# Stick-breaking attention with its stages moved apart, its sums from split operands, and seven of the weight halves made on GpSimd

## The chip, the core and the metric

The kernel runs on one core of a Trainium2 chip. The metric is the device time of one execution in microseconds. The work is spread over the engines that the profile calls PE (TensorE, matrix products), ACT (ScalarE), DVE (VectorE), POOL (GpSimd) and SP (SyncE, here the queue that issues the DMAs). Each engine works through its own queue in order and waits on semaphores where it needs what another engine makes.

## What is computed

Two transformer blocks run one after the other on 256 tokens of width 1024, in float32. The part that matters here is the first block's stick-breaking attention, with 8 heads of width 64, and the RWKV branch beside it. The reference, cut to that:

```python
def stick_breaking_attention(q, k, v):
    for i in range(S // Q_BLOCK):                 # Q_BLOCK = 128, S = 256
        ...
        z = jnp.einsum('bqhd,bkhd->bhqk', qb, kb).astype(jnp.float32) * scale
        strict = s_idx < t_idx
        log_fail = jnp.where(strict, jax.nn.log_sigmoid(-z), 0.0)
        after = lax.cumsum(log_fail, axis=3, reverse=True) - log_fail
        w = jnp.where(strict, jnp.exp(jax.nn.log_sigmoid(z) + after), 0.0)
        outs.append(jnp.einsum('bhqk,bkhd->bqhd', w.astype(vb.dtype), vb))

def first_block(x, ...):
    h = rms_norm(x, norm_mix_pre[l])
    proj = h @ w_in[l]                            # 1024 x 5376
    ...
    o_sb = stick_breaking_attention(q, k, v)
    o_rw = rwkv7_time_mix(p_rw, ...)              # a recurrence over the tokens
    merged = gates[..., :D] * (o_sb @ w_sb_out[l]) + gates[..., D:] * (o_rw @ w_rw_out[l])
    ...
```

## The kernel before

**Weights.** Every weight matrix is streamed in slabs of 128 x 1024 floats (four times 128 rows by 256 columns). The method `slab` loads one (a DMA into `wraw`, 512 KB), rounds it on ACT to `whi` (line 182), and takes the rest on DVE as `wlo = wraw - whi` (line 183). Buffers: three of `wraw`, four each of `whi` and `wlo`; `fetch` keeps three slabs ahead of PE. A block is what PE does with one slab: 24 matmuls of 256 columns, three products (hi by hi, hi by lo, lo by hi) for each of eight pairs. The input matrix comes as `w_rw` (14 slabs), `w_sb` (12 slabs: two pairs each for q, k and v in that order) and `w_gate` (16 slabs), two slabs to a group of 256 output columns, the lower half being rows 512 to 1023 (odd slab numbers). Here they are called sb0 to sb11 and g0 to g15.

**Weaving.** `weave` takes a generator, and each call of `next_slab`, so each block, advances it by one step. While PE works on the v slabs sb8 to sb11 and the gate slabs g0 to g7 (twelve blocks, numbered 0 to 11 here), the steps are the attention's: `sb_scores(j)`, `sb_weights(j)`, `sb_values(j)` for four pairs of heads j. With `staggered(..., apart=2)` scores stand ahead of blocks 0, 2, 4, 6, weights ahead of 2, 4, 6, 8, and values ahead of 4, 6, 8, 10; at a block with all three, values come first and scores last.

**The stages.** `sb_scores` makes the masked logits of a pair in PSUM (`pz`, two buffers of the pool `zz`), then |z|, exp and log on ACT (Abs, Exp, Ln), then on DVE `zm = max(z, 0) + log(...)` (line 784). `sb_weights` adds to the same `pz` the suffix sums of `zm` by two matmuls of 384 and two of 128 columns against the constants `suffix` and `negones`, all plain float32, and takes the exponential on ACT into `ab`. `sb_values` multiplies with v into `po`, copies it to `of` and splits that into `sh`, `sl`.

**Beside it** DVE inverts 16 x 16 triangles for the RWKV branch: fifteen pairs of `pr` and `TF` (lines 718 and 719) in a chain that starts when the matrix `Q` has landed, then two steps of `rows` (`prw`, lines 736 and 739), the first two products against `Q`, the other two against `low`, which goes out and back by DMA after ACT's copy `aux` (line 722) of the finished `TF`. A scheduler sets the order of each engine's queue from the program; what results is a fixed row of instructions on each engine.

Of the kernel before, what the change touches and what calls it, by code (L numbers as in the profile page):

```python
# [43 lines left out]
for _n, _c in VECS:  # L44
# [47 lines left out]
class Net:  # L92
    def __init__(self, ctx, tc, io):
        self.tc, self.nc, self.io = tc, tc.nc, io
        self.last_table = None
        self.queue, self.ready = [], []
        self.t2 = 3
        self.side = None
        nc = self.nc
        pool = lambda name, bufs=1, **k: ctx.enter_context(tc.tile_pool(name=name, bufs=bufs, **k))  # L100
        self.keep = pool("keep")
        self.pr = pool("wraw", 3)
        self.ph = pool("whi", 4)
# [70 lines left out]
    def slab(self, name, i):  # L174
        nc = self.nc
        off, k0, m, c0 = slabs(*WEIGHTS[name])[i]
        w = m * width(name)
        raw = self.pr.tile([P, SW], F32, tag="wraw", name="wraw")
        hi = self.ph.tile([P, SW], F32R, tag="whi", name="whi")
        lo = self.pl.tile([P, SW], F32R, tag="wlo", name="wlo")  # L180
        nc.sync.dma_start(raw[:, :w], self.io[name][off:off + P * w].rearrange("(p n) -> p n", p=P))
        nc.scalar.copy(hi[:, :w], raw[:, :w])  # L182
        nc.vector.tensor_sub(lo[:, :w], raw[:, :w], hi[:, :w].bitcast(F32))  # L183
        h3 = hi[:, :w].rearrange("p (k c) -> p k c", k=m)
        l3 = lo[:, :w].rearrange("p (k c) -> p k c", k=m)
        return h3, l3, k0, m
# [231 lines left out]
def first(n):  # L418
    nc, tc = n.nc, n.tc
    with ExitStack() as ctx:  # L420
# [81 lines left out]
        n.normed(tmp, xp, r, "norm_mix_pre", n.xh, n.xl)  # L502
        shifted(2, kf, 2, r)
        start.close()
        b4 = ctx.enter_context(tc.tile_pool(name="b4", bufs=8))


        n.table("sigmoid_and_others")
# [183 lines left out]

        def sb_v(g):
            ps = n.group("w_sb", 4 + g, n.xh, n.xl, tok=True)
            nc.vector.tensor_copy(vs_[:, :, g * 256:(g + 1) * 256], ps)

# [58 lines left out]
            for q in range(2):  # L755
                nc.vector.tensor_mul(MG[h][q][:, :, 0, :], MG[h][q][:, :, 0, :], low)

        sbf = tmp.tile([P, 384], F32, tag="t30", name="sbf", bufs=4)
        o, w = COFF["sbmask"]
        nc.scalar.dma_start(sbf, n.io["cst"][:, o:o + w])  # L760
        sbm = one.tile([P, 384], BF16, name="sbm")
        nc.scalar.copy(sbm, sbf)
        idb = one.tile([P, P], BF16, name="idb")
        nc.scalar.copy(idb, n.c("ident"))
        sh = b4.tile([P, NP, T], F32R, tag="b4", name="sh")
# [6 lines left out]
        def sb_scores(j):  # L772
            p = pz[j] = n.zz("pz")
            for o, kc, qc in ((slice(0, T), slice(0, P), slice(0, T)), (slice(T, T + P), slice(P, T), slice(P, T))):
                for r_, rr in enumerate(half):
                    n.mm(p[:, r_, o], ks[rr, j, kc], qs[rr, j, qc], start=kc.start == 0)
            for r_ in range(2):
                n.mm(p[:, r_, :384], idb, sbm, start=False)
            z = tmp.tile([P, 2, 384], F32, tag="t30", name="zm", bufs=4)
            ab = tmp.tile([P, 2, 384], F32, tag="t30", name="ab", bufs=4)  # L780
            nc.scalar.activation(ab, p[:, :, :384], AF.Abs)
            n.act(ab, ab, AF.Exp, scale=-1.0)
            n.act(ab, ab, AF.Ln, bias=n.one)
            nc.vector.scalar_tensor_tensor(z, p[:, :, :384], 0.0, ab, op0=ALU.max, op1=ALU.add)
            zm[j] = z, ab

        def sb_weights(j):
            p, (z, ab) = pz[j], zm[j]
            for r_ in range(2):
                n.mm(p[:, r_, :384], n.c("suffix"), z[:, r_, :], start=False)  # L790
            for r_ in range(2):
                n.mm(p[:, r_, P:T], n.c("negones"), z[:, r_, T:384], start=False)
            n.act(ab, p[:, :, :384], AF.Exp)

        def sb_values(j):
            wt = zm[j][1]
            po = n.sx("po")
            for t, o, wc in ((0, slice(0, T), slice(0, T)), (1, slice(P, T), slice(T, 384))):
                for r_, rr in enumerate(half):
                    i = 2 * j + r_  # L800
                    n.mm(po[rr, o], vs_[:, t, 64 * i:64 * i + 64], wt[:, r_, wc], start=t == 0)
            of = tmp.tile([P, T], F32, tag="c2", name="of", bufs=3)
            nc.vector.tensor_copy(of, po[:, :T])
            n.split(of, sh[:, j, :], sl[:, j, :])

        early.close()
        n.psum(sb, zz=2, sx=2)
        n.weave(staggered(NP, sb_values, sb_weights, sb_scores, apart=2))
        sb_v(0)
        sb_v(1)  # L810
        gr = [B(f"gate{i}") for i in range(4)]

        def gate(g, final):

            i, h = g // 2, 2 * (g % 2)
            ps = n.group("w_gate", g, n.xh, n.xl)
            if final:
                sig(g, ps)
            else:
                nc.scalar.copy(gr[i][:, h:h + 2, :], ps)  # L820
# [23 lines left out]
        def solve(h):  # L844
# [114 lines left out]
        def normalized():  # L959
# [479 lines left out]
```

## Time and profile before

| | |
|---|---|
| median of 3 runs | 851.95 us (851.76 to 854.29) |
| the profiled execution's own time | 853.44 us |
| its span, first to last instruction | 851.7 us |
| PE busy | 829.5 us (97%), 6508 matmuls |
| DVE busy | 565.3 us (66%), 790 instructions |
| ACT busy | 464.9 us (55%), 714 instructions |
| POOL busy | 5.4 us (1%), 14 instructions |
| chain that ended last, by engine | PE 90%, DVE 5%, DMA 2%, ACT 2%, issue 1% |
| granted clock of TensorE, mean | 0.994 |

A matmul's end is modelled, so a busy PE isn't PE at its peak; what counts is when each group of matmuls starts. The busy shares are means over stages with different limits: over the whole span DVE is busy two thirds of the time, but between 105 and 143 us it is hardly ever idle. The timeline merges like instructions that follow one another; its first two columns are the start and the time from there to the end, and square brackets hold the idle time before and what ended it.

### The profile page before, as it was taken

To read this page: it belongs to the slowest core of one execution; us is meant where nothing else is said; L and a number is where in the kernel's file an instruction comes from. 1 tells how busy PE (TensorE), PEld (TensorE's weight loads), DVE (VectorE), ACT (ScalarE), POOL (GpSimd) and SP (SyncE) were. 2 spreads that over 40 slices of the span, in tenths; PEclk is the share of its full clock that TensorE was granted. 3 is DMA by queue.
4 is the path that set the end of the run, shared out by engine and by line. 5 is a ranking of instruction groups with operands and counts; after the bars stand their busy time and mean duration, and the time that the engine had idled before them with its cause. 6 is when DMAs were issued, how large, how long until landed. Compare 5 with 4: busy or idle time off the path is not lost.

```text
span 851.7 us, 15759 instructions
## 1 busy us (share of the span) xinstructions
PE 829.5 (97%) x6508; PEld 788.4 (93%) x6508; DVE 565.3 (66%) x790; ACT 464.9 (55%) x714; POOL 5.4 (1%) x14
## 2 busy tenths in 40 slices
PE   5999998999999999999999999999999999999996
PEld 5798987999999999999999998999999999988884
DVE  6858689455888776666545876689576666654543
ACT  6497355643577654445445657457455565553432
POOL 0001001000000000000000000000000000000000
PEclk9999999999999999999999999999999999999999
DMA  8434443542464765555555564455524555556551
GB/s 283 149 133 159 136 130 117 160 140 87 145 251 144 225 189 183 195 177 197 173 187 186 158 202 149 148 174 184 188 95 153 176 172 177 193 178 193 179 193 50
DMA packets 44631, 142.88 MB, mean 168 GB/s; under 512 B 8976, under 2 KB 9744, under 8 KB 44304
## 3 DMA queue, kind: packets, MB, share of 16 engines
q1 hardware_dynamic: 43840, 139.25, 50.7%
q10 hardware_dynamic: 720, 2.63, 0.8%
q8 instruction: 51, 0.84, 0.4%
q14 instruction: 20, 0.16, 0.1%
HBM read 139.17 MB, written 2.69 MB: 167 GB/s over the span
## 4 chain that ended last, share of the span: by engine, by line
PE 90%; DVE 5%; DMA 2%; ACT 2%; issue 1%; SPq 0%; ACTq 0%; DVEq 0%
PE mm L247 68%; PE mm L262 11%; DMA wraw<-in_w_rw 2%; PE pz L262 2%; DVE wlo L183 1%; PE po L262 1%; ACT whi L182 1%; PE px L262 1%; PE mgnh L262 1%; PE nv L262 1%; DVE prw L736 1%; PE kv L247 1%; PE ssum L262 1%; DVE pr L718 1%; DVE TF L719 0%
## 5 line engine op out<-in xcount | busy, mean ns | idle before, releaser
L183 DVE TENSOR_TENSOR wlo<-wraw,whi 128x1024 fp32r<-128x1024 f32 x254 | 308.2, 1215 | 198.8 <-ACT whi L182 197.3
L182 ACT CAST whi<-wraw 128x1024 fp32r<-128x1024 f32 x254 | 264.8, 1044 | 291.5 <-PE mm L247 174.9
L247 PE MATMUL mm<-xh,whi 128*128 128x256 f32 x1120 | 319.3, 285 | 0.0
L247 PE MATMUL mm<-xh,wlo 128*128 128x256 f32 x1120 | 316.1, 282 | 1.8 <-DVE wlo L183 1.8
L247 PE MATMUL mm<-xl,whi 128*128 128x256 f32 x1120 | 316.1, 282 | 0.0
L247 PEld LDWEIGHTS mm<-xh,whi 128*128 128x128 f32 x1120 | 212.0, 189 | 3.8 <-issue 2.2
L247 PEld LDWEIGHTS mm<-xh,wlo 128*128 128x128 f32 x1120 | 211.8, 189 | 2.9 <-DVE wlo L183 2.2
L247 PEld LDWEIGHTS mm<-xl,whi 128*128 128x128 f32 x1120 | 211.8, 189 | 0.9 <-issue 0.7
L262 PE MATMUL mm<-whi,ah 128*128 128x512 f32 x128 | 50.6, 395 | 0.0
L262 PE MATMUL mm<-whi,al 128*128 128x512 f32 x128 | 50.6, 395 | 0.0
L262 PE MATMUL mm<-wlo,ah 128*128 128x512 f32 x128 | 50.6, 395 | 0.0
L247 PE MATMUL mm<-fh,whi 128*128 128x256 f32 x176 | 49.1, 279 | 0.0
L247 PE MATMUL mm<-fl,whi 128*128 128x256 f32 x176 | 49.1, 279 | 0.0
L247 PE MATMUL mm<-fh,wlo 128*128 128x256 f32 x176 | 49.1, 279 | 0.0
L247 PEld LDWEIGHTS mm<-fl,whi 128*128 128x128 f32 x176 | 33.1, 188 | 0.0
L247 PEld LDWEIGHTS mm<-fh,wlo 128*128 128x128 f32 x176 | 33.1, 188 | 0.0
L247 PEld LDWEIGHTS mm<-fh,whi 128*128 128x128 f32 x176 | 33.1, 188 | 0.0
L262 PEld LDWEIGHTS mm<-whi,al 128*128 128x128 f32 x128 | 24.1, 188 | 5.8
L262 PEld LDWEIGHTS mm<-wlo,ah 128*128 128x128 f32 x128 | 24.1, 188 | 5.8
L262 PEld LDWEIGHTS mm<-whi,ah 128*128 128x128 f32 x128 | 24.1, 188 | 5.7
L247 PE MATMUL rw<-gh,whi 128*128 128x256 f32 x48 | 14.2, 296 | 9.0 <-ACT whi L182 9.0
L247 PE MATMUL mm<-memh,whi 128*128 128x256 f32 x64 | 18.8, 294 | 0.0
(349 smaller groups left out, 1379.9 us busy)
## 6 DMA issues: line engine op xcount, KB each, us to landing
wraw<-in_w_up SPq DMA_DIRECT2D x32, 512.0 KB, 3.5
wraw<-in_w_down SPq DMA_DIRECT2D x32, 512.0 KB, 4.3
wraw<-in_w_in SPq DMA_DIRECT2D x24, 512.0 KB, 4.2
wraw<-in_w_ffn_gate SPq DMA_DIRECT2D x22, 512.0 KB, 3.8
wraw<-in_w_ffn_up SPq DMA_DIRECT2D x22, 512.0 KB, 3.3
wraw<-in_w_ffn_down SPq DMA_DIRECT2D x20, 512.0 KB, 3.5
wraw<-in_w_gate SPq DMA_DIRECT2D x16, 512.0 KB, 3.3
wraw<-in_w_kv_mem SPq DMA_DIRECT2D x16, 512.0 KB, 3.3
```

The lines of the kernel that those rows point to most:

```text
L182: nc.scalar.copy(hi[:, :w], raw[:, :w])
L183: nc.vector.tensor_sub(lo[:, :w], raw[:, :w], hi[:, :w].bitcast(F32))
L247: self.nc.tensor.matmul(ps[:, c, :], lhsT, rhs, start=first, stop=last, skip_group_check=True)
L262: self.nc.tensor.matmul(out, lhsT, rhs, start=start, stop=stop, skip_group_check=True)
L718: nc.vector.tensor_mul(pr[:, :, :, :t + 1], tri[:, :, :, :t + 1], q)
L736: nc.vector.tensor_mul(pr, left[:, r:r + 4, :].rearrange("p r (o i) -> p r o i", o=1).to_broadcast([P, 4, 16, 16]), right.rearrange("p (o ...
```

## The change

1. **GpSimd makes `wlo` of seven slabs**: sb3, sb5, sb7, sb9, sb11, g1 and g3. DVE makes the others as before.
2. **The stages stand further apart**: scores ahead of blocks 0, 2, 4, 6 as before, weights ahead of 3, 5, 7, 9 (three blocks after their scores instead of two), values ahead of 5, 7, 9, 11.
3. **The sums take split operands**: the result of line 784 goes into `ab` itself and is split into `zhi` (a cast on ACT) and `zlo` (a subtraction on DVE); the suffix sums are eight fp32r matmuls in place of four float32 ones, against `sums`, an fp32r copy of the two constants, whose columns hold only 0 and -1. The exponential goes to a new tile `wt`.
4. **Small moves**: the copies of v from PSUM go from DVE to ACT; `po` is split without the copy `of`; the constants are loaded in another order (the load at the start on ACT's queue is 640 columns wide in place of 384, the one on SP's queue 960 in place of 1216); the pool `t30` has six buffers for four and `b4` seven for eight, and the gate tiles are taken when first needed.

```diff
 class Net:
+        self.others = {"w_sb": (3, 5, 7, 9, 11), "w_gate": (1, 3)}
...
         nc.scalar.copy(hi[:, :w], raw[:, :w])
-        nc.vector.tensor_sub(lo[:, :w], raw[:, :w], hi[:, :w].bitcast(F32))
+        engine = nc.gpsimd if i in self.others.get(name, ()) else nc.vector
+        engine.tensor_sub(lo[:, :w], raw[:, :w], hi[:, :w].bitcast(F32))
...
         def sb_v(g):
-            nc.vector.tensor_copy(vs_[:, :, g * 256:(g + 1) * 256], ps)
+            nc.scalar.copy(vs_[:, :, g * 256:(g + 1) * 256], ps)
...
+        sums = tmp.tile([P, 256], F32R, tag="t1", name="sums", bufs=1)
+        nc.scalar.copy(sums, sbf[:, 384:])
...
         def sb_scores(j):
-            z = tmp.tile([P, 2, 384], F32, tag="t30", name="zm", bufs=4)
-            ab = tmp.tile([P, 2, 384], F32, tag="t30", name="ab", bufs=4)
+            ab = tmp.tile([P, 2, 384], F32, tag="t30", name="ab", bufs=6)
+            hi = tmp.tile([P, 2, 384], F32R, tag="t30", name="zhi", bufs=6)
+            lo = tmp.tile([P, 2, 384], F32R, tag="t30", name="zlo", bufs=6)
             nc.scalar.activation(ab, p[:, :, :384], AF.Abs)
             n.act(ab, ab, AF.Exp, scale=-1.0)
             n.act(ab, ab, AF.Ln, bias=n.one)
-            nc.vector.scalar_tensor_tensor(z, p[:, :, :384], 0.0, ab, op0=ALU.max, op1=ALU.add)
+            nc.vector.scalar_tensor_tensor(ab, p[:, :, :384], 0.0, ab, op0=ALU.max, op1=ALU.add)
+            n.split(ab, hi, lo)
...
         def sb_weights(j):
             for r_ in range(2):
-                n.mm(p[:, r_, :384], n.c("suffix"), z[:, r_, :], start=False)
+                for z in (hi, lo):
+                    n.mm(p[:, r_, :384], sums[:, :P], z[:, r_, :], start=False)
             for r_ in range(2):
-                n.mm(p[:, r_, P:T], n.c("negones"), z[:, r_, T:384], start=False)
-            n.act(ab, p[:, :, :384], AF.Exp)
+                for z in (hi, lo):
+                    n.mm(p[:, r_, P:T], sums[:, P:], z[:, r_, T:384], start=False)
+            wt = zm[j] = tmp.tile([P, 2, 384], F32, tag="t30", name="wt", bufs=6)
+            n.act(wt, p[:, :, :384], AF.Exp)
...
         def sb_values(j):
-            of = tmp.tile([P, T], F32, tag="c2", name="of", bufs=3)
-            nc.vector.tensor_copy(of, po[:, :T])
-            n.split(of, sh[:, j, :], sl[:, j, :])
+            n.split(po[:, :T], sh[:, j, :], sl[:, j, :])
...
-        n.weave(staggered(NP, sb_values, sb_weights, sb_scores, apart=2))
+        def attention():
+            for b in range(2 * NP + 4):
+                for stage, first in ((sb_values, 5), (sb_weights, 3), (sb_scores, 0)):
+                    j = (b - first) // 2
+                    if (b - first) % 2 == 0 and 0 <= j < NP:
+                        stage(j)
+                yield
+        n.weave(attention())
```

The queues change with it. PE, before, at block 4 (ahead of g0): values of pair 0, weights of pair 1, scores of pair 2, then the mask's matmuls and the block (`po` is the values' PSUM tile, `pz` the logits').

```order
L262 MATMUL po<-ab,vs 64x256 x2
L262 MATMUL po<-ab,vs 64x128 x2
L262 MATMUL pz<-zm,cst 128x384 x2
L262 MATMUL pz<-zm,cst 128x128 x2
L262 MATMUL pz<-qs,ks 128x256 x2
L262 MATMUL pz<-qs,ks 128x128 x2
```

PE now, at block 5 (ahead of g1), the values of pair 0 and the weights of pair 1:

```order
L265 MATMUL po<-wt,vs 64x256 x2
L265 MATMUL po<-wt,vs 64x128 x2
L265 MATMUL pz<-zhi,sums 128x384
L265 MATMUL pz<-zlo,sums 128x384
L265 MATMUL pz<-zhi,sums 128x384
L265 MATMUL pz<-zlo,sums 128x384
L265 MATMUL pz<-zhi,sums 128x128
L265 MATMUL pz<-zlo,sums 128x128
L265 MATMUL pz<-zhi,sums 128x128
L265 MATMUL pz<-zlo,sums 128x128
```

The scores of pair 2 stay ahead of block 4, now alone, with the weights of pair 0 one block ahead of them instead of two. They write the `pz` buffer of pair 0, so they wait for ACT's exponential of pair 0.

ACT, before, from the Abs of pair 0 (line 781) to the Ln of pair 1. The exponential of pair 0 into `ab` (from `pz`, line 145) stands ahead of the Abs of pair 1 and of the copy `aux`:

```order
L781 ACTIVATE ab<-pz 128x768
L145 ACTIVATE ab<-ab 128x768
L145 ACTIVATE ab<-ab,eps 128x768
L182 CAST whi<-wraw 128x1024 x2
L145 ACTIVATE ab<-pz 128x768
L781 ACTIVATE ab<-pz 128x768
L145 ACTIVATE ab<-ab 128x768
L722 COPY aux<-TF 128x128
L145 ACTIVATE ab<-ab,eps 128x768
```

ACT now, from the cast `zhi` of pair 0 to the exponential `wt` of pair 0:

```order
L269 CAST zhi<-ab 128x768
L184 CAST whi<-wraw 128x1024
L698 COPY vs<-mm 128x2x256
L788 ACTIVATE ab<-pz 128x768
L725 COPY aux<-TF 128x128
L147 ACTIVATE ab<-ab 128x768
L147 ACTIVATE ab<-ab,eps 128x768
L184 CAST whi<-wraw 128x1024
L269 CAST zhi<-ab 128x768
L147 ACTIVATE wt<-pz 128x768
```

The exponential of pair 0 has moved behind `aux`, behind Exp and Ln of pair 1 and behind the cast `zhi` of pair 1. In the same way the exponential of pair 1, for which the scores of pair 3 wait, now stands behind `zhi` of pair 2.

DVE, before, from line 784 for pair 1 to line 784 for pair 2:

```order
L784 SCALAR_TENSOR_TENSOR zm<-pz,ab 128x768
L183 TENSOR_TENSOR wlo<-wraw,whi 128x1024
L736 TENSOR_TENSOR prw<-TF,Q 128x1024
L695 COPY vs<-mm 128x2x256
L739 TENSOR_REDUCE aux<-prw 128x64
L803 COPY of<-po 128x256
L736 TENSOR_TENSOR prw<-TF,Q 128x1024
L267 TENSOR_TENSOR sl<-of,sh 128x256
L739 TENSOR_REDUCE aux<-prw 128x64
L183 TENSOR_TENSOR wlo<-wraw,whi 128x1024
L736 TENSOR_TENSOR prw<-aux,low_1299 128x1024
L784 SCALAR_TENSOR_TENSOR zm<-pz,ab 128x768
```

DVE now, the same stretch:

```order
L791 SCALAR_TENSOR_TENSOR ab<-pz,ab 128x768
L186 TENSOR_TENSOR wlo<-wraw,whi 128x1024
L739 TENSOR_TENSOR prw<-TF,Q 128x1024
L270 TENSOR_TENSOR zlo<-ab,zhi 128x768
L742 TENSOR_REDUCE aux<-prw 128x64
L739 TENSOR_TENSOR prw<-TF,Q 128x1024
L742 TENSOR_REDUCE aux<-prw 128x64
L739 TENSOR_TENSOR prw<-aux,low_1299 128x1024
L791 SCALAR_TENSOR_TENSOR ab<-pz,ab 128x768
```

One `wlo`, the copies `vs` and `of` and the early `sl` have left the stretch, one `zlo` has come in, and line 784's operation for pair 2 still stands behind all of the first `rows` step. Ahead of it, in the chain of `pr` and `TF`, two of four `wlo` and the copy `vs` have left, and line 784's operation for pair 0 and its `zlo` stand in place of one `zm`.

## Rows read from the trace of the kernel before

**Rows 1.** The page, part 1: busy time, share of the span, instructions.

```profile
PE 829.5 (97%) x6508; PEld 788.4 (93%) x6508; DVE 565.3 (66%) x790; ACT 464.9 (55%) x714; POOL 5.4 (1%) x14
```

**Rows 2.** Chain that ended last, in order of time: start us, us, what.

```profile
142.80 5.67 PE mm L247 x48
...
151.21 5.68 PE mm L247 x48
...
156.89 0.80 PE po L262 x8
...
157.69 5.87 PE mm L247 x48
...
163.55 1.78 PE px L262 x16
...
754.48 88.21 PE mm L262 x378
```

**Rows 3.** Timeline of PE, two gaps at 24 to 38 and 115 to 143.

```profile
33.27 0.49 PE L247 MATMUL mm<-xh,wlo 128*128 128x256 f32 x1 [1.76 <-DVE wlo L183]
...
115.70 1.90 PE L262 MATMUL pz<-zm,cst 128*128 128x384 f32 x8
...
118.58 0.41 PE L247 MATMUL mm<-whi,xh 128*128 128x256 f32 x1
...
125.51 2.00 PE L262 MATMUL pz<-zm,cst 128*128 128x384 f32 x8 [0.23 <-DVE zm L784]
...
137.94 2.57 PE L262 MATMUL pz<-zm,cst 128*128 128x384 f32 x8 [2.67 <-DVE zm L784]
...
142.39 0.53 PE L247 MATMUL mm<-xh,whi 128*128 128x256 f32 x1
```

**Rows 4.** Stretches: us, PE (x), PEld (x), DVE, ACT, POOL busy, PEclk, DMA, GB/s.

```profile
32.00:36.00 4.00, 2.73 (x13) 2.73 (x14) 4.00 (x8) 0.00 (x0) 0.00 (x0) 0.67 0.39 129
...
140.00:142.00 2.00, 2.00 (x11) 1.40 (x9) 2.00 (x3) 0.00 (x0) 0.00 (x0) 0.50 0.42 104
```

**Rows 5.** Timeline of DVE in the attention's stretch.

```profile
104.29 1.23 DVE L183 TENSOR_TENSOR wlo<-wraw,whi 128x1024 fp32r<-128x1024 f32 x1 [1.57 <-ACT whi L182]
...
105.69 0.19 DVE L718 TENSOR_TENSOR pr<-TF,Q 128x32 f32<-128x32 f32 x1
...
107.13 1.23 DVE L183 TENSOR_TENSOR wlo<-wraw,whi 128x1024 fp32r<-128x1024 f32 x1 [0.23 <-ACT whi L182]
...
118.01 0.68 DVE L695 COPY vs<-mm 128x512 f32<-128x512 f32 x1
...
121.06 0.62 DVE L718 TENSOR_TENSOR pr<-TF,Q 128x240 f32<-128x240 f32 x1
...
122.82 0.42 DVE L719 TENSOR_REDUCE TF<-pr 128x16 f32<-128x256 f32 x1
...
124.50 0.96 DVE L784 SCALAR_TENSOR_TENSOR zm<-pz,ab 128x768 f32<-128x768 f32 x1 [1.26 <-PE mm L247]
...
130.19 0.42 DVE L803 COPY of<-po 128x256 f32<-128x256 f32 x1
...
136.95 0.94 DVE L784 SCALAR_TENSOR_TENSOR zm<-pz,ab 128x768 f32<-128x768 f32 x1
```

**Rows 6.** Timeline of ACT in the same stretch.

```profile
95.95 1.05 ACT L182 CAST whi<-wraw 128x1024 fp32r<-128x1024 f32 x1 [0.98 <-ACT Y L682]
...
123.33 0.30 ACT L722 COPY aux<-TF 128x128 f32<-128x128 f32 x1 [2.72 <-DVE TF L719]
...
131.80 0.85 ACT L145 ACTIVATE ab<-ab 128x768 f32<-128x768 f32 x1
```

**Rows 7.** Timeline of POOL: a memset of one slab's size.

```profile
74.46 0.96 POOL L842 MEMSET SA<- 128x1024 f32 x1 [7.13 <-DVE bon L627]
```

**Rows 8.** Timeline of SP's queue, ahead of the chain of triangles.

```profile
98.28 0.35 SPq L181 DMA_DIRECT2D wraw<-in_w_sb  x1
...
99.29 1.17 SPq L703 DMA_DIRECT2D Q<-scrM  x2
```

More of the change, by code (lines that the diff above doesn't have):

```diff
@@ L51 @@
     ("ident", 128), ("blk", 128), ("wmask", 256), ("kmask", 256),
-    ("suffix", 128), ("negones", 128), ("low32", 128), ("eye64", 64),
-    ("eyeT", 512), ("sbmask", 384), ("dil", 512),
+    ("low32", 128), ("eye64", 64),
+    ("eyeT", 512), ("sbmask", 384), ("suffix", 128), ("negones", 128), ("dil", 512),
 ]
@@ L504, in first @@
         start.close()
-        b4 = ctx.enter_context(tc.tile_pool(name="b4", bufs=8))
+        b4 = ctx.enter_context(tc.tile_pool(name="b4", bufs=7))
         n.table("sigmoid_and_others")
@@ L756, in first @@
                 nc.vector.tensor_mul(MG[h][q][:, :, 0, :], MG[h][q][:, :, 0, :], low)
-        sbf = tmp.tile([P, 384], F32, tag="t30", name="sbf", bufs=4)
+        sbf = tmp.tile([P, 640], F32, tag="t30", name="sbf", bufs=6)
         o, w = COFF["sbmask"]
-        nc.scalar.dma_start(sbf, n.io["cst"][:, o:o + w])
+        nc.scalar.dma_start(sbf, n.io["cst"][:, o:o + 640])
         sbm = one.tile([P, 384], BF16, name="sbm")
-        nc.scalar.copy(sbm, sbf)
+        nc.scalar.copy(sbm, sbf[:, :384])
+        sums = tmp.tile([P, 256], F32R, tag="t1", name="sums", bufs=1)
+        nc.scalar.copy(sums, sbf[:, 384:])
         idb = one.tile([P, P], BF16, name="idb")
@@ L783, in sb_scores @@
             n.act(ab, ab, AF.Ln, bias=n.one)
-            nc.vector.scalar_tensor_tensor(z, p[:, :, :384], 0.0, ab, op0=ALU.max, op1=ALU.add)
-            zm[j] = z, ab
+            nc.vector.scalar_tensor_tensor(ab, p[:, :, :384], 0.0, ab, op0=ALU.max, op1=ALU.add)
+            n.split(ab, hi, lo)
+            zm[j] = hi, lo
         def sb_weights(j):
-            p, (z, ab) = pz[j], zm[j]
+            p, (hi, lo) = pz[j], zm[j]
             for r_ in range(2):
-                n.mm(p[:, r_, :384], n.c("suffix"), z[:, r_, :], start=False)
+                for z in (hi, lo):
+                    n.mm(p[:, r_, :384], sums[:, :P], z[:, r_, :], start=False)
             for r_ in range(2):
-                n.mm(p[:, r_, P:T], n.c("negones"), z[:, r_, T:384], start=False)
-            n.act(ab, p[:, :, :384], AF.Exp)
+                for z in (hi, lo):
+                    n.mm(p[:, r_, P:T], sums[:, P:], z[:, r_, T:384], start=False)
+            wt = zm[j] = tmp.tile([P, 2, 384], F32, tag="t30", name="wt", bufs=6)
+            n.act(wt, p[:, :, :384], AF.Exp)
         def sb_values(j):
-            wt = zm[j][1]
+            wt = zm[j]
             po = n.sx("po")
@@ L801, in sb_values @@
                     n.mm(po[rr, o], vs_[:, t, 64 * i:64 * i + 64], wt[:, r_, wc], start=t == 0)
-            of = tmp.tile([P, T], F32, tag="c2", name="of", bufs=3)
-            nc.vector.tensor_copy(of, po[:, :T])
-            n.split(of, sh[:, j, :], sl[:, j, :])
+            n.split(po[:, :T], sh[:, j, :], sl[:, j, :])
[6 more added lines that the diff above has]
+                yield
         early.close()
         n.psum(sb, zz=2, sx=2)
-        n.weave(staggered(NP, sb_values, sb_weights, sb_scores, apart=2))
+        n.weave(attention())
         sb_v(0)
         sb_v(1)
-        gr = [B(f"gate{i}") for i in range(4)]
+        gr = [None] * 4
         def gate(g, final):
             i, h = g // 2, 2 * (g % 2)
+            if h == 0:
+                gr[i] = B(f"gate{i}")
             ps = n.group("w_gate", g, n.xh, n.xl)
@@ L860, in solve @@
                     n.mm(py[:, i * P:(i + 1) * P], MG[h][q][:, i, 0, :], xs[q][:, i, :], start=i == 0)
-                ys[q] = tmp.tile([P, 4, P], F32, tag="t30", name="y1", bufs=4)
+                ys[q] = tmp.tile([P, 4, P], F32, tag="t30", name="y1", bufs=6)
                 (nc.vector.tensor_copy if q else nc.scalar.copy)(
@@ L981, in normalized @@
                 n.mm(ps, n.c("blk"), pv[i])
-                lv = tmp.tile([P, 2, T], F32, tag="t30", name="lgv", bufs=4)
+                lv = tmp.tile([P, 2, T], F32, tag="t30", name="lgv", bufs=6)
                 n.act(lv, ps.rearrange("p (c t) -> p c t", c=2), AF.Ln, bias=n.gneps, scale=1.0 / HD)
```

## The prediction

> **What bounds the kernel now.** I read the page first: PE is busy for 829.5 of 851.7 us [rows 1], so only PE's own work and the places where PE waits can move the time. Next the chain that ended last: in the stretch that the change touches it is made of blocks, 48 matmuls in 5.68 us, so 2.84 a slab and 0.118 a matmul of 256 columns, until the first product of the recurrence (`px`) starts at 163.55 [rows 2]. Behind that PE runs without a wait that I could find, so what is won or lost ahead of `px` is the forecast for the whole.
>
> Then PE's timeline. It waits twice for line 784 of DVE: 0.23 us ahead of the weights of pair 1 and 2.67 us ahead of those of pair 2 [rows 3]. After the second gap the weights and scores take 4.45 us (137.94 to 142.39), where they took 2.88 at 115.70 to 118.58 [rows 3]: the granted clock is at 0.50, the lower of its two levels, at 140 to 142 [rows 4]. That is 1.57 us on top. A wait of 1.76 us at 33.27 was also followed by a lower clock, 0.67 in the mean of its four us [rows 3, 4]. So the stretch holds 2.9 us of waiting and 1.6 of slow clock.
>
> The cause of the long gap is DVE's row. The chain of `pr` and `TF` runs from 105.69 to 123.24 (122.82 and 0.42), ACT copies `aux` and makes the Ln of pair 1, and from line 784 for pair 1 (124.50) to the same for pair 2 (136.95) DVE works through 12.45 us of `rows`, `wlo` and copies [rows 5, 6].
>
> **The change part by part.**
>
> *Sums on PE.* Four float32 matmuls take 1.90 us (115.70) [rows 3]; 0.05 of it overlaps what follows. The eight fp32r ones aren't in this trace as such. An fp32r matmul of 512 columns takes 0.233 us (88.21 by 378) and one of 256 takes 0.118 [rows 2], so one of 384 about 0.175; one of 128 lies between 0.06 (half) and 0.118 (the weight load sets it). That gives 0.94 to 1.17; I take 1.05, 0.8 less in each of four places. It counts only where PE isn't waiting anyway: behind the last gap, twice.
>
> *DVE's chain.* Of its 17.55 us I take out four `wlo` (1.23 each, the first at 107.13), one `zm` (0.96) and one copy of v (0.68), 6.6 in all [rows 5]; I put in two `wlo`, line 784 for pair 0 and its `zlo`, which I price as line 784 (same 768 columns), 4.4. So 15.4.
>
> *Its start.* `Q` goes out behind the load of sb10 on SP's queue (98.28, then 99.29) [rows 8], and that load now waits for GpSimd's `wlo` of sb7 instead of DVE's. The cast of sb7 ends at 97.0 [rows 6]. No row shows a subtraction on GpSimd. From below: a memset of the same size takes 0.96 us [rows 7]. From above: two reads and a write, each as long as that, 2.9. At 0.96 `Q` goes out as before, and the chain, no longer behind the `wlo` of sb9 (104.29), can start up to 0.9 earlier; at 2.9 `Q` goes out 1.0 later and eats that. I take the upper end, so the start stays at 105.7 and the chain ends at E = 121.1, 2.1 earlier than before.
>
> *The new wait.* This speaks against the change. The scores of pair 2 reuse the buffer of pair 0, so PE waits for the exponential of pair 0, and that is now queued on ACT behind `aux`, Exp and Ln of pair 1, a cast and `zhi` of pair 1. Behind E that is 0.1, then 0.30 for `aux`, 0.85 each for Exp and Ln, 1.05 for the cast, 0.85 each for `zhi` and the exponential (priced as the Exp at 131.80) [rows 6]: 4.9, so 126.0. PE is there at 115.7 + 1.0 (scores of pair 1) + 2.84 + 1.05 + 2.84 = 123.4. A gap of 2.6 opens where there was 0.23; the three blocks between scores and weights gain nothing at this place.
>
> *The second wait.* The scores of pair 3 wait for the exponential of pair 1, behind `zhi` of pair 2, behind line 784 for pair 2, still behind the first `rows` step. From Ln of pair 1 (E + 2.1) DVE needs the old 12.45 less the copy of v, `of`, a `sl` of its size (0.42) and a `wlo`, 2.75 in all, plus 0.96 for `zlo`: 10.7 to its start, 0.96 for itself [rows 5]. Then `zhi` and the exponential, 1.7, and a little for semaphores: E + 15.5 = 136.6. PE, released at 126.0, gets there after 1.0 + 2.84 + 0.8 (values, 156.89) + 1.05 + 2.84, at 134.5 [rows 2]. So 2.1 us of waiting remain. Queued behind it are only PE's own later blocks, whose slabs are made by then.
>
> *To the end of the stretch.* From 136.6 PE has scores 1.0, six blocks 17.2 (5.67, 5.68 and 5.87), three values 2.4 and two sums 2.1, 22.7 in all: `px` at 159.3 instead of 163.55 [rows 2]. That is 4.25 us won if the clock stays up, 2.7 if it drops at the second gap as before, 5.2 if the chain starts 0.9 earlier. If it drops at the first gap instead, PE arrives late at the second by less than that gap, which costs nothing. I take the middle, 3.4.
>
> *What costs nothing.* The weights of pair 0 need `zlo` of pair 0, two pairs of `pr` and `TF` ahead of E, so 2.2 earlier (121.06 to 123.24) [rows 5], at 118.9; PE is there at 119.5. Without that 0.6 the first gap moves one block forward, and E still decides. The copies of v and the casts `zhi` go to ACT, whose waits on DVE are longer than they are. Buffers of `b4` are first rewritten behind the stretch. The larger load at the start is offset by a smaller one on SP's queue; it could cost some tenths.
>
> **The rivals.**
>
> *GpSimd holds DVE up (slower).* GpSimd's memsets read nothing, so this trace can't show whether a GpSimd instruction that reads stops a DVE operation with two inputs from SBUF, as `pr`, `prw`, `wlo` and `zlo` are. If it does for its whole length, sb9 (from 104.3) delays the chain's start by 1.5 at a length of 2.9, and sb11, g1 and g3 each stop DVE for 2.9 less the 0.3 of a `TF` in between: 9.3 in all, on the path that sets both gaps. Then `px` is 5.0 later than before, 6.6 with the slow clock: 857 to 858.6, say 857.5. At a length of 0.96 it would be 2.0, and the kernel still faster. It decides from 4.25 us of delay, or 2.7 with a clock drop. The Trainium skill, "SBUF — State Buffer", section "Who interferes with whom", says just this: VectorE with two SBUF inputs and a reading GpSimd instruction exclude one another, and the second blocks until the first is done. By that rule the change loses; no run here shows it yet. The Trainium skill, "GPSIMD Engine Reference", section "3. Performance versus the Vector engine", has 4497 ns for 2048 elements, so an estimate of 2.25 us a slab, and a delay of about 6.7 us: 854.4 to 856. Against the rival: sb3, sb5 and sb7 fall where DVE works from PSUM or is idle, and where DVE holds the port first, GpSimd is the one that waits, which costs little, since slabs are made well ahead.
>
> *Partial hold-up (no change).* Both engines slow each other a little, 2 to 4 us in all: 850 to 853.5, say 852. That the moved work simply changes nothing ends here too.
>
> *Both gaps close (much faster).* If PE alone sets the stretch, the 2.9 of waiting, 1.6 of clock and four times 0.8 are all won, 7.6 us: 844.3. It needs E before 118.6, 2.5 earlier than I find, and line 784 for pair 2 far earlier in DVE's row.
>
> **How the numbers follow.** The sum is made on the profiled execution (span 851.7, own time 853.44); its own time is 1.5 above the median of the runs shown, so I apply the difference to the median, 851.95. Forecast 848.5, chance 0.50, its own range 846.8 to 849.3. Hold-up 857.5, 0.28. No change 852, 0.15. Both gaps closed 844.3, 0.07. The range reaches from 846.0 to 857.0: it leaves out the last case and the upper half of the hold-up. About 0.3% is what a measurement can tell from no change, so faster means below 849.4: 0.42 of the forecast's 0.50 and the 0.07, 0.49. Within 0.3%: 0.08 of the forecast and 0.11 of the no-change case, 0.19. Slower: 0.28 and 0.04, 0.32.
>
> **What would show it.** Right: PE waits on the ACT exponential ahead of the scores of pairs 2 and 3, about 2.6 and 2.1 us, and no longer on line 784; the chain of triangles ends near 121; the sums take about 1.05; `px` starts near 159 to 161. GpSimd's hold-up: `pr`, `prw` or `zlo` starts late behind a GpSimd `wlo` while nothing else is missing, or lasts well over its old time. Wrong in another way: PE waits for POOL at one of the seven slabs, or for `zlo` of pair 0 by several us.

## The result and the profile after

The changed kernel takes 858.76 us (median of 6 runs, 857.54 to 862.51), the kernel before 852.0 beside it: ratio 1.0077, 95% interval [1.0064, 1.0091]. It is slower by 6.8 us, where 848.5 was forecast and 846 to 857 given as the range. The profiled execution took 859.07, with a span of 857.3 (853.44 and 851.7 before), so the two traces are only 5.6 us apart. In the lines of the profile after, a line of the code is numbered three higher than before.

The page, part 1, and the group of GpSimd's new operation (line, engine, operation, xcount | busy us, mean ns | idle before):

```profile
PE 828.9 (97%) x6508; PEld 788.9 (92%) x6508; DVE 570.0 (66%) x781; ACT 469.3 (55%) x721; POOL 24.2 (3%) x21
```

```profile
L186 POOL TENSOR_TENSOR wlo<-wraw,whi 128x1024 fp32r<-128x1024 f32 x7 | 18.9, 2705 | 47.3 <-ACT whi L184 44.8 <-DVE kap L588 2.6
```

VectorE has nine instructions fewer than in [rows 1] in sum (seven subtractions of 1.2 us are among those that left, four `zlo` of 0.95 among those that came), and yet it is busy for 4.7 us longer. GpSimd's seven take 18.9 us; something was added on VectorE too. The timelines of the two engines, side by side, show what. GpSimd's seven (start us, us, engine, line, operation, [idle before <-releaser]):

```profile
68.46 2.82 POOL L186 TENSOR_TENSOR wlo<-wraw,whi 128x1024 fp32r<-128x1024 f32 x1 [2.57 <-DVE kap L588]
77.35 2.51 POOL L186 TENSOR_TENSOR wlo<-wraw,whi 128x1024 fp32r<-128x1024 f32 x1 [6.08 <-ACT whi L184]
97.49 2.39 POOL L186 TENSOR_TENSOR wlo<-wraw,whi 128x1024 fp32r<-128x1024 f32 x1 [17.62 <-ACT whi L184]
104.35 2.41 POOL L186 TENSOR_TENSOR wlo<-wraw,whi 128x1024 fp32r<-128x1024 f32 x1 [2.67 <-ACT whi L184]
110.02 2.40 POOL L186 TENSOR_TENSOR wlo<-wraw,whi 128x1024 fp32r<-128x1024 f32 x1 [3.26 <-ACT whi L184]
120.97 3.67 POOL L186 TENSOR_TENSOR wlo<-wraw,whi 128x1024 fp32r<-128x1024 f32 x1 [8.56 <-ACT whi L184]
131.21 2.74 POOL L186 TENSOR_TENSOR wlo<-wraw,whi 128x1024 fp32r<-128x1024 f32 x1 [6.57 <-ACT whi L184]
```

VectorE in the attention's stretch, the chain of triangles and what follows it:

```profile
106.33 0.48 DVE L721 TENSOR_TENSOR pr<-TF,Q 128x32 f32<-128x32 f32 x1
...
110.39 2.25 DVE L721 TENSOR_TENSOR pr<-TF,Q 128x112 f32<-128x112 f32 x1
...
112.99 0.41 DVE L721 TENSOR_TENSOR pr<-TF,Q 128x128 f32<-128x128 f32 x1
...
120.94 0.95 DVE L270 TENSOR_TENSOR zlo<-ab,zhi 128x768 fp32r<-128x768 f32 x1
121.80 0.58 DVE L721 TENSOR_TENSOR pr<-TF,Q 128x240 f32<-128x240 f32 x1
...
122.86 2.28 DVE L721 TENSOR_TENSOR pr<-TF,Q 128x256 f32<-128x256 f32 x1
125.17 0.42 DVE L722 TENSOR_REDUCE TF<-pr 128x16 f32<-128x256 f32 x1
...
131.63 3.13 DVE L270 TENSOR_TENSOR zlo<-ab,zhi 128x768 fp32r<-128x768 f32 x1
```

The `pr` of 112 columns takes 2.25 us, the larger one of 128 right behind it 0.41. It starts 0.37 after GpSimd's subtraction of sb11 (110.02 to 112.42) and ends 0.22 after it. In the same way the `pr` at 122.86 ends half a microsecond behind the subtraction of g1 (to 124.64), and the `zlo` at 131.63, 3.13 long where the one at 120.94 took 0.95, ends 0.8 behind that of g3 (to 133.95). No row is missing and no semaphore is named: the time is inside VectorE's own rows. In the other direction the subtraction of g1, started beside the `zlo` of 120.94, takes 3.67 where an undisturbed one takes 2.4: `zlo` and the `pr` right behind it (121.80, 0.58) both take their usual time, and GpSimd waits for them.

So the chain of triangles ends at E = 125.59 (125.17 and 0.42), not at 123.24 as before [rows 5] nor at the 121.1 of the prediction. What PE makes of it, its timeline:

```profile
121.94 0.44 PE L265 MATMUL pz<-zlo,sums 128*128 128x384 f32 x1 [1.49 <-DVE zlo L270]
...
130.25 1.42 PE L265 MATMUL pz<-qs,ks 64*128 64x256 f32 x8 [4.28 <-ACT wt L147]
...
143.72 1.23 PE L265 MATMUL pz<-qs,ks 64*128 64x256 f32 x8 [2.74 <-ACT wt L147]
...
168.75 1.95 PE L265 MATMUL px<-R,TT 128*128 128x128 f32 x16
```

Three waits, 8.5 us in all, where [rows 3] had 2.9 in two; `px` starts at 168.75, 5.4 later than before (163.39 in this view; the 163.55 of [rows 2] is the chain's, which has 168.91 now). And each of the two long gaps is followed by a lower clock (the column behind POOL is PEclk; stretches of 4 us from just ahead of the gap's end):

```profile
129.00:133.00 4.00, 2.75 (x14) 2.22 (x15) 4.00 (x3) 3.16 (x5) 1.79 (x1) 0.69 0.49 164
143.00:147.00 4.00, 3.29 (x18) 2.80 (x19) 4.00 (x5) 3.31 (x5) 0.95 (x1) 0.65 0.00 0
```

### The profile page after: what moved, and what is told of

It is laid out like the page before. It is cut to its first block, busy times and chain, and to the rows that moved or that the text cites. A ratio compares the mean times of both kernels' runs of the same rounds, so it can differ in the third digit from the quotient of the medians.

```text
span 857.3 us, 15758 instructions
## 1 busy us (share of the span) xinstructions
PE 828.9 (97%) x6508; PEld 788.9 (92%) x6508; DVE 570.0 (66%) x781; ACT 469.3 (55%) x721; POOL 24.2 (3%) x21
## 4 chain that ended last, share of the span: by engine, by line
PE 87%; DVE 6%; ACT 3%; DMA 2%; issue 1%; SPq 0%; ACTq 0%; DVEq 0%
PE mm L250 65%; PE mm L265 11%; DVE wlo L186 2%; PE pz L265 1%; DMA wraw<-in_w_rw 1%; DVE pr L721 1%; PE po L265 1%; PE rw L250 1%; PE px L265 1%; PE mgnh L265 1%; ACT whi L184 1%; PE nv L265 1%; PE ssum L265 1%; PE kv L250 1%; DMA wraw<-in_w_sb 1%
## 5 line engine op out<-in xcount | busy, mean ns | idle before, releaser
L186 DVE TENSOR_TENSOR wlo<-wraw,whi 128x1024 fp32r<-128x1024 f32 (+1 forms) x247 | 299.6, 1215 | 197.9 <-ACT whi L184 196.1
L186 POOL TENSOR_TENSOR wlo<-wraw,whi 128x1024 fp32r<-128x1024 f32 x7 | 18.9, 2705 | 47.3 <-ACT whi L184 44.8
```

The costliest lines, as they stand in the source:

```text
L186: engine.tensor_sub(lo[:, :w], raw[:, :w], hi[:, :w].bitcast(F32))
```

## The experiments

Two theories. Theory 1: a GpSimd instruction that reads SBUF stops a VectorE operation with two SBUF inputs for as long as it lasts, and the change loses where such an operation stands on the path. Theory 2: the loss is the new wait that the change builds, for a buffer of scores whose exponential is queued late on ACT. All times below are medians, with the ratio to the kernel before on the same chip.

**All lower halves on VectorE.** The rest of the change stays.

```
-        self.others = {"w_sb": (3, 5, 7, 9, 11), "w_gate": (1, 3)}
+        self.others = {}
```

> The changed kernel with its seven subtractions back on VectorE; stages, split sums and small moves stay. Theory 1 (a GpSimd subtraction stops VectorE's operations with two inputs from SBUF for its length, and this is the loss): VectorE gets up to seven times 1.14 us of work back but loses no time to blocking, so the first product of the recurrence starts near 163 to 164.5 and the time is 851 to 853.5 us. Theory 2 (GpSimd costs nothing; the scores' new wait for the exponential is the loss): the wait stays, VectorE has more to do, 858 to 861 us.

848.80, ratio 0.9963 [0.9951, 0.9975]. It is faster than both kernels, and below what theory 1 gave. Of the three waits one is left (engine, line waited for: us in total, times, longest), and the last `pr` has its old length:

```profile
PE pz L265 <- ACT wt L147: 1.9, 1, 1.9
```

```profile
122.92 0.64 DVE L721 TENSOR_TENSOR pr<-TF,Q 128x256 f32<-128x256 f32 x1
```

Putting the seven subtractions on GpSimd costs 10.0 us; the rest of the change gains 3. The time is below the expected 851 to 853.5, though the chain of triangles, with its subtractions back, ends at 124.76, only 0.8 earlier than in after. PE waits so little because ACT's order is another one (its rows stand further down): the scores of pair 2 are released 1.5 us behind the chain's end, where after has 4.66. So this run alone does not tell the theories apart: with the subtractions the late exponential of theory 2 has gone too. The next three runs separate them.

**GpSimd's part alone.** The kernel before, and only these lines:

```
+        self.others = {"w_sb": (3, 5, 7, 9, 11), "w_gate": (1, 3)}
...
+        engine = nc.gpsimd if i in self.others.get(name, ()) else nc.vector
+        engine.tensor_sub(lo[:, :w], raw[:, :w], hi[:, :w].bitcast(F32))
```

> The kernel before with the first part alone: GpSimd makes the lower half of the seven slabs, stages and sums as before. Theory 1: the chain of triangles ends 1.5 to 3 us later than before although three subtractions have left it, operations of VectorE behind a GpSimd subtraction show 2 us too much, and the time is 853.5 to 856 us. Theory 2: the gap of 2.67 us ahead of the sums of pair 2 closes, 846 to 849.5 us.

856.48, ratio 1.0058 [1.0039, 1.0078]: 4.7 slower, a little over theory 1's range, and far from theory 2's. VectorE's timeline has two stretched rows in the chain, which ends at 126.55, 3.3 later than before (1.5 to 3 were expected). PE waits 6.03 for line 787 (784 before) of pair 0, whose sums it reached without a wait in [rows 3] (115.70). That line starts at 121.12 where it started at 114.41 before: of these 6.7 us, 4.3 are the two stretched rows (0.33 and 0.49 before), 1.55 the later start of the chain (107.24), the rest the order of VectorE's queue. PE waits for no exponential here:

```profile
110.38 2.54 DVE L721 TENSOR_TENSOR pr<-TF,Q 128x96 f32<-128x96 f32 x1
...
117.31 2.55 DVE L721 TENSOR_TENSOR pr<-TF,Q 128x192 f32<-128x192 f32 x1
```

```profile
122.12 3.78 PE L265 MATMUL pz<-zm,cst 128*128 128x384 f32 x8 [6.03 <-DVE zm L787]
```

**Stages two blocks apart.** The kernel after with the old spacing, GpSimd's part and split sums kept.

```
-        n.weave(attention())
+        n.weave(staggered(NP, sb_values, sb_weights, sb_scores, apart=2))
```

> The changed kernel with the stages two blocks apart as before; GpSimd, split sums and small moves stay. Theory 1: the chain of triangles still ends near 125 us, TensorE waits for the split of pair 1 and pair 2 in place of the exponential, 855 to 858 us. Theory 2: the wait for the exponential is gone and with it the loss, 846 to 850 us.

862.47, ratio 1.0126 [1.0105, 1.0148], which neither theory expected. With the sums a block earlier PE meets the delayed `zhi` and `zlo` instead of the exponential: it waits 4.94 and 2.99 for `zhi` and 1.39 for `zlo`. The mean clock in the 32 us around is 0.79:

```profile
119.58 0.57 PE L265 MATMUL pz<-zhi,sums 128*128 128x384 f32 x1 [4.94 <-ACT zhi L269]
...
146.25 0.44 PE L265 MATMUL pz<-zhi,sums 128*128 128x384 f32 x1 [2.99 <-ACT zhi L269]
```

```profile
118.00:150.00 32.00, 25.87 (x156) 22.59 (x156) 28.04 (x24) 16.54 (x22) 8.65 (x5) 0.79 0.21 73
```

So the spacing does not lose anything; it takes 3.7 us off the price of the rest. The wait that theory 2 blames is gone here and the kernel is slower still.

**GpSimd busy, but reading nothing.** The kernel after, with each subtraction on GpSimd replaced by three memsets of the same tile.

```
-        engine.tensor_sub(lo[:, :w], raw[:, :w], hi[:, :w].bitcast(F32))
+            for _ in range(3):
+                nc.gpsimd.memset(lo[:, :w].bitcast(F32), 0.0)
```

> The changed kernel with each of GpSimd's seven subtractions replaced by three memsets of the same tile, which read nothing and take about 2.9 us together, so GpSimd is busy as long at the same places; the lower halves of these slabs are left out of the sums (zeros). Theory 1 (it is the reading that blocks): no operation of VectorE is stretched, the chain of triangles ends near 121 to 122 us, TensorE waits about 2.5 and 2 us for the exponentials, and the time is 847 to 851 us, as forecast. Theory 2, or a cost of GpSimd's being busy or late: 857 to 860 us as with the subtractions.

848.98, ratio 0.9967 [0.9954, 0.998]. GpSimd is busy as long as before (20.0 us against 18.9), and beside a triple of memsets `wlo` and `zlo` take their usual time. GpSimd, then VectorE at the same place:

```profile
114.47 2.98 POOL L187 MEMSET wlo<- 128x1024 f32 x3 [3.90 <-PE mm L253]
```

```profile
114.72 1.22 DVE L189 TENSOR_TENSOR wlo<-wraw,whi 128x1024 fp32r<-128x1024 f32 x1
...
116.15 0.95 DVE L273 TENSOR_TENSOR zlo<-ab,zhi 128x768 fp32r<-128x768 f32 x1
```

What holds VectorE up is that GpSimd reads, not that it works. But this comparison does not hold everything else equal: the memsets wait for no cast and keep no raw tile, so SP's queue is freer and `Q` lands some 3.6 us earlier than in after. The last experiment below brings the wait for the cast back, though not the hold on the raw tile. ACT's order is that of after: the scores of pair 2 start 4.72 behind the chain's end here and 4.66 there. So the 9.9 us between the two starts of `px` can be split along the path. The rows of the memset kernel, of VectorE and PE:

```profile
102.68 0.19 DVE L724 TENSOR_TENSOR pr<-TF,Q 128x32 f32<-128x32 f32 x1
...
118.78 0.42 DVE L725 TENSOR_REDUCE TF<-pr 128x16 f32<-128x256 f32 x1
```

```profile
135.35 0.93 PE L268 MATMUL pz<-qs,ks 64*128 64x256 f32 x8 [2.25 <-ACT wt L147]
...
158.85 1.95 PE L268 MATMUL px<-R,TT 128*128 128x128 f32 x16
```

| part of the path | memsets | after | difference |
|---|---|---|---|
| start of the chain of triangles | 102.68 | 106.33 | 3.65 |
| the chain | 16.52 | 19.26 | 2.74 |
| its end to the scores of pair 3 | 16.15 | 18.13 | 1.98 |
| from there to `px` | 23.50 | 25.03 | 1.53 |

The two middle parts, 4.7 us, are where the stretched rows stand (the chain of the memset kernel also holds a wait of 0.93 for a cast, which that of after does not); the last is the slow stretch behind the second gap. The first is the earlier start. So the memsets do not show 9.8 us of hold-up. They also miss their own expectation in part: the chain ends at 119.20 instead of 121 to 122, and PE waits 1.45 and 2.25 instead of 2.5 and 2.

**Where the subtraction stands.** The seven were divided: the four early ones (sb3, sb5, sb7, sb9) on GpSimd alone, then the three late ones (sb11, g1, g3) alone.

```
+        self.others = {"w_sb": (3, 5, 7, 9)}
```

> The kernel after with four of the seven subtractions left on GpSimd (sb3, sb5, sb7, sb9) and sb11, g1 and g3 back on VectorE. Theory 1 (a GpSimd subtraction costs what it adds to a two-input VectorE operation that stands on the path): in the trace of after the hold-ups of sb3 and sb5 were 0.6 and 0.3, those of sb7 and sb9 fell where VectorE waited for Q anyway, so 848.8 + 0.9 = 849.7, in 848 to 851.5. Theory 2 (each GpSimd subtraction costs about the same wherever it stands): 848.8 + 4/7 of 10.0 = 854.5, in 853 to 856.

```
+        self.others = {"w_sb": (11,), "w_gate": (1, 3)}
```

> The other half: sb11, g1 and g3 on GpSimd, the four early ones back on VectorE. Theory 1: these three stood beside `pr`, `pr` and `zlo` on the path and stretched them by 1.9, 1.65 and 2.2, so 848.8 + 5.75 = 854.5, in 852.5 to 858, and over the run with the early slabs by at least 3. Theory 2: 848.8 + 3/7 of 10.0 = 853.1, and below the run with the early slabs by about 1.4.

Early: 851.59, ratio 1.0004 [0.999, 1.0018]. Late: 855.69, ratio 1.0045 [1.0026, 1.0064]. Three late ones cost 6.9 over the kernel without any, four early ones 2.8, together 9.7 of the 10.0. The order is theory 1's; an equal price for each would have put the early ones above. The early ones came out just over theory 1's range. Their stretched rows do lie ahead of the chain. The expectation had read the hold-ups of sb3 and sb5 as 0.6 and 0.3; the rows show 2.2 and 1.5 (the same rows take 0.42 and 1.66 without GpSimd), and the chain's wait for `Q` takes most of it up:

```profile
68.78 2.60 DVE L494 TENSOR_TENSOR v<-y,pad 128x256 f32<-128x256 f32 x1
...
78.06 3.13 DVE L641 SCALAR_TENSOR_TENSOR gb<-gb,vec,g 128x256 f32<-128x256 f32 x4
```

but ACT's order changed with them. The first fence is ACT's timeline of the kernel without GpSimd, the second that of the one with the early four:

```profile
124.47 0.83 ACT L269 CAST zhi<-ab 128x768 fp32r<-128x768 f32 x1 [2.84 <-DVE ab L791]
125.20 0.29 ACT L725 COPY aux<-TF 128x128 f32<-128x128 f32 x1
125.40 0.80 ACT L147 ACTIVATE wt<-pz 128x768 f32<-128x768 f32 x1
```

```profile
124.38 0.30 ACT L725 COPY aux<-TF 128x128 f32<-128x128 f32 x1 [2.46 <-DVE TF L722]
124.59 1.04 ACT L184 CAST whi<-wraw 128x1024 fp32r<-128x1024 f32 x1
125.53 0.83 ACT L269 CAST zhi<-ab 128x768 fp32r<-128x768 f32 x1
126.27 0.80 ACT L147 ACTIVATE wt<-pz 128x768 f32<-128x768 f32 x1
```

With the early four, a cast and `zhi` stand between `aux` and the exponential that PE waits for, and PE's wait is 3.19 instead of 1.87, though the chain ends earlier, at 124.35 against 124.76. That is 1.3 of the 2.8; the two profiled executions themselves are only 1.0 apart in span, so what makes up the rest of the medians' difference I can't say.

The late ones carry ACT's order too (there the scores of pair 2 start 3.84 behind the chain's end), so their 6.9 are not the hold-up alone. They show in one place how the two engines take turns. GpSimd, then VectorE:

```profile
130.28 3.61 POOL L186 TENSOR_TENSOR wlo<-wraw,whi 128x1024 fp32r<-128x1024 f32 x1 [6.81 <-ACT whi L184]
```

```profile
128.81 1.97 DVE L739 TENSOR_TENSOR prw<-TF,Q 128x1024 f32<-128x1024 f32 x1
130.69 0.96 DVE L270 TENSOR_TENSOR zlo<-ab,zhi 128x768 fp32r<-128x768 f32 x1
131.56 1.22 DVE L742 TENSOR_REDUCE aux<-prw 128x64 f32<-128x1024 f32 x1
132.81 2.98 DVE L739 TENSOR_TENSOR prw<-TF,Q 128x1024 f32<-128x1024 f32 x1
```

GpSimd's row begins at 130.28, under the first `prw`; that one and the `zlo` right behind it take their usual 1.97 and 0.96, and GpSimd's row grows to 3.61, 1.2 over its usual 2.4. So it ran for its 2.4 from about 131.5, when `zlo` was done. Under it the reduce, with one input, takes its usual 1.22. The `prw` with two inputs starts at 132.81 and takes 2.98 instead of the 1.97 of the first: GpSimd ended at 133.89, 1.1 into it.

**Where the 3 us come from.** First without GpSimd and with the old spacing (both edits as above, split sums kept), then without GpSimd, three blocks apart, and plain fp32 sums.

> No subtraction on GpSimd (as the first experiment, 848.8), and the stages two blocks apart as in the kernel before, sums still from split operands. If the spacing is what gives the 3.1 us that the rest of the change gained, the wait of PE for the upper and lower halves of pair 0 comes back at the third scores: 851 to 853. If the gain comes from the sums and the smaller moves: 848 to 850. With GpSimd on, the spacing was worth 3.7, which would give 852.5.

```
-            n.split(ab, hi, lo)
-            zm[j] = hi, lo
+            zm[j] = (ab,)
...
-                for z in (hi, lo):
+                for z in zs:
```

> No subtraction on GpSimd, stages three blocks apart, and the sums from plain fp32 operands as in the kernel before (1.83 us on PE a pair, where split ones took 1.2), so that the casts `zhi` and the subtractions `zlo` (0.95 us each on VectorE) are gone. If the split is what gains: four pairs by 0.63, 2.5 us later, 850.5 to 852. If the split pays for its shorter matmuls with the two operations it puts between `ab` and the sums: 847 to 849.5, no worse than 848.8.

Two blocks apart: 852.40, ratio 1.0015 [1.0002, 1.0028], the gain gone. Plain sums three blocks apart: 848.44, ratio 0.9969 [0.9957, 0.9981], all of it there. Then the spacing on the kernel before (the copies of `vs` and `of` are back on VectorE too; the pool sizes, the tile `wt` and the load of the constants stay as in after):

```
-            nc.scalar.copy(vs_[:, :, g * 256:(g + 1) * 256], ps)
+            nc.vector.tensor_copy(vs_[:, :, g * 256:(g + 1) * 256], ps)
...
-            n.split(po[:, :T], sh[:, j, :], sl[:, j, :])
+            of = tmp.tile([P, T], F32, tag="c2", name="of", bufs=3)
+            nc.vector.tensor_copy(of, po[:, :T])
+            n.split(of, sh[:, j, :], sl[:, j, :])
```

> The kernel before with the stages three blocks apart and nothing else of the change that orders work: plain fp32 sums, all lower halves on VectorE, the copy of `vs` and the copy `of` back on VectorE (the pool sizes and the load of the sums' constants stay as in after). If the spacing carries the whole gain that was left without GpSimd: 848 to 849.5, the same as the run with plain sums (848.44). If the smaller moves carry a part (two copies of `vs` and four of `of` off VectorE, about 0.4 to 0.9 us each, those ahead of the third scores on the path): 849.5 to 851.5.

848.26, ratio 0.9966 [0.9954, 0.9978]. In that trace one wait of 0.6 is left of all:

```profile
PE pz L265 <- ACT wt L147: 0.6, 1, 0.6
```

and in its ACT row the exponential stands straight behind `aux`:

```profile
123.90 0.30 ACT L725 COPY aux<-TF 128x128 f32<-128x128 f32 x1 [3.11 <-DVE TF L722]
124.11 0.80 ACT L147 ACTIVATE wt<-pz 128x768 f32<-128x768 f32 x1
```

The medians in one table:

| lower halves, sums | two blocks apart | three blocks apart |
|---|---|---|
| VectorE, plain | 851.8 (before) | 848.26; with the smaller moves 848.44 |
| VectorE, split | 852.40 | 848.80 |
| seven on GpSimd, plain | 856.48 | not run |
| seven on GpSimd, split | 862.47 | 858.76 (after) |

The spacing gains 3.4 to 3.7. The split sums cost 0.4 to 0.6, within what the intervals allow as nothing. GpSimd costs 4.7 with plain sums and 10.0 or 10.1 with split ones. Why twice as much: split sums put `zlo`, an operation with two SBUF inputs, where line 784 reads PSUM, and in after it is `zlo` that g3 holds for 2.2 us. ACT's late exponential is another part: 4.66 behind the chain's end in after, 1.5 in the kernel without GpSimd. How the difference divides between the two was not measured.

**One input read.** The kernel after, with GpSimd copying the upper half in place of subtracting: the wait for the cast is as in after, but the raw tile is not read.

```
-        engine.tensor_sub(lo[:, :w], raw[:, :w], hi[:, :w].bitcast(F32))
+            nc.gpsimd.tensor_copy(lo[:, :w], hi[:, :w].bitcast(F32))
```

> The kernel after with each of the seven GpSimd subtractions replaced by a GpSimd copy of the upper half into the tile of the lower half: it waits for the same cast and reads one input in place of two (the lower halves of those seven slabs are left out). If what holds VectorE up is GpSimd's reading from SBUF as such: two-input operations of VectorE that meet a copy are stretched to about its end, and the time lies above 851 if the copy lasts as long as the subtraction (2.4), in 850 to 856. If only GpSimd operations with two inputs hold VectorE up: no stretched row, and 847 to 850, as with the memsets (848.98).

852.51, ratio 1.0004 [0.9989, 1.002]: 3.7 over the kernel without GpSimd. An undisturbed copy takes 1.04 us. Six of the seven stretched a two-input row; the seventh (128.44) met only a reduce. The first fence is one of GpSimd's copies, the second three of the rows that copies stretched:

```profile
105.27 1.04 POOL L186 CAST wlo<-whi 128x1024 fp32r<-128x1024 f32 x1 [4.03 <-ACT whi L184]
```

```profile
105.52 0.86 DVE L723 TENSOR_TENSOR pr<-TF,Q 128x48 f32<-128x48 f32 x1
...
111.34 0.93 DVE L723 TENSOR_TENSOR pr<-TF,Q 128x144 f32<-128x144 f32 x1
...
119.85 1.43 DVE L723 TENSOR_TENSOR pr<-TF,Q 128x240 f32<-128x240 f32 x1
```

One read is enough. The 3.7 us are not all hold-up: ACT's order is that of after (4.67 from the chain's end to the scores of pair 2), not that of the kernel without GpSimd. The 6.3 us to after are not all length either, since `Q` lands 1.3 earlier here. How the price goes with the length is not shown.

## Why the prediction was wrong, step by step

**The step that failed is GpSimd's price on VectorE, which the sum had at nothing.** The forecast took the subtractions as free for VectorE (chance 0.50) and the hold-up as the rival (0.28). The hold-up is what happens. `px` was forecast at 159.3 and started at 168.75. Of these 9.4 us, 6.05 are rows on the path that GpSimd stretched (0.3, 1.9 and 1.65 in the chain, 2.2 in `zlo`), 1.8 are the slow stretch behind the second gap, 0.6 the later start of the chain, and some 1.0 small things.

The case for free had two arguments. One, that sb3, sb5 and sb7 fall where VectorE works from PSUM or is idle, does not hold: each stretched a row (in the trace of after to 2.59 for 0.42, 3.10 for 1.66 and 2.50 for 0.69). They cost little because these rows lie ahead of the chain's wait for `Q`. The other, that GpSimd would be the one to wait where VectorE came first, is true (3.67 and 3.61 instead of 2.4) and no help: GpSimd gets its turn behind the operations under way and queued without a gap (two of them in each of these rows), and the next two-input operation then waits for the whole subtraction.

The rule that the prediction named was right as far as these runs test it. A copy with one input stretched `pr`, memsets did not, a reduce with one input went on under a subtraction. The Trainium skill, "SBUF — State Buffer", section "Who interferes with whom", says that a VectorE instruction with two SBUF inputs contends with a GpSimd instruction that reads SBUF and not with one that only writes, and that `tensor_reduce` never contends on this chip: the traces agree, with 2.25 for 0.4 us, 0.95 beside memsets, and 1.22 under a subtraction.

**The length.** Bounded from 0.96 to 2.9, measured 2.34 to 2.41 where nothing disturbs it. The Trainium skill, "GPSIMD Engine Reference", section "3. Performance versus the Vector engine", gave the estimate of 2.25; it is 4 to 7% low.

**E.** Forecast 121.1, measured 125.59. The 4.5 are: the start, 106.33 instead of 105.7, 0.6; the first `pr`, beside sb9, 0.48 for the 0.19 of [rows 5], 0.3; sb11 on the `pr` of 110.39, 1.9; g1 on that of 122.86, 1.65 (2.28 against 0.62 to 0.64). The start is not hold-up: `Q` went out at 100.92, 1.6 later than in [rows 8], where the prediction had 1.0 even for a subtraction of 2.9; it goes out 1.01 behind the load of sb10 in both traces, so the whole delay of the load, which waits for GpSimd's `wlo` of sb7 (to 99.88), is passed on. The prediction's delay of 1.5 by sb9 did not come, since VectorE was waiting for `Q` anyway. With the 2.2 of the `zlo` behind E the hold-up on the path is 6.05; the prediction had 9.3 from the upper bound of the length. By the Trainium skill's figure for the length it had about 6.7.

**The waits.** Their mechanism was right. The first was to be released 4.9 behind E; it was 4.66 (130.25). The second 15.5 behind E; it was 18.1 (143.72), of which 2.2 is the held `zlo`. That E was late made the gaps 4.28 and 2.74 instead of 2.6 and 2.1, and `zlo` of pair 0 opened a third, 1.49, where the prediction had a margin of 0.6; that one costs nothing of its own, since PE still waits for E behind it.

**To the end.** From the second release to `px` 22.7 was forecast and 25.0 measured. The scores took 1.5 for 1.0 and the first slab 4.1 for 2.84 at the lower clock, together 1.8; the sums took 1.20 (136.73 to 137.93) for the 1.05 forecast, 0.3 for two; the rest is 0.2. So the hold-up was smaller than the 9.3 of the upper bound, and yet the time came to 858.76, just above where that bound had put it (857 to 858.6). That is partly luck: the second slow stretch and the later start made up for 2.4, and the medians are 6.8 apart where the traces are 5.6, a difference that no trace here explains. By the Trainium skill's figure the rival had been 854.4 to 856, which was too low for the same reasons.

**The forecast without the hold-up** was 848.5, and the kernel in which GpSimd works without reading takes 848.98, the one without GpSimd 848.80. The number was nearly right for these kernels, but by luck: with memsets the chain starts 3.0 earlier than the forecast had it, and without GpSimd it ends 3.7 later than the 121.1 but the exponential is not late. The sums' 0.8 us a pair and the smaller moves give nothing that shows (848.80 with, 848.26 without them), which fits that each split puts `zhi` and `zlo` ahead of the sums. The sentence that the three blocks "gain nothing at this place" was wrong: the spacing is worth 3.4 to 3.7 us, with the rest of the kernel the same (852.40 and 848.80, 862.47 and 858.76). It takes PE off line 784 in both places, and what takes its place, the exponential behind E, is short when ACT runs it straight behind `aux`: 1.1 us behind E (123.82 to 124.91) instead of 4.66. That order is not written in the change; it follows from what else is queued, and with the subtractions on GpSimd it comes out the other way.

**The chances.** Slower had 0.32. The trace of before had no row in which GpSimd reads, so it could not decide; a rule that named this very pair of operands deserved more than 0.28.

## What to carry to other kernels

Before work goes to an idle GpSimd, list what VectorE runs in the same microseconds: if rows with two SBUF inputs stand there on the path, a GpSimd operation that reads can stretch one of them by nearly its own length, here up to 2.2 us to save 1.2. Memsets of the same size stretched nothing. Of a change with several parts run each part alone: here the spacing held the gain, and with plain sums and all lower halves on VectorE it gives 848.26 us, 3.5 below the kernel before and 10.5 below after. And compare the order of the queues between two runs before putting their difference down to one cause: here moving work off VectorE also moved an exponential on ACT by some 3 us.

## What was not expected of the hardware

The hold-up is nowhere shown as waiting: the profile adds it to the duration of VectorE's row (2.25, 2.28, 3.13 us) and of GpSimd's (3.67), so idle times and releasers look clean and only the duration of one shape against another gives it away. And a copy of 1.04 us on GpSimd, of one input, stretched `pr` of 48, 144 and 240 columns by 0.65, 0.5 and 0.8 us, so short GpSimd operations cost less but are not free.
